# A decay tile of its own, and three loaded rows instead of four, in a Hymba step

## The chip, the cores and the metric

The kernel runs on one core of a Trainium2 chip. The metric is the device time of that core in microseconds (us); lower is better. Work is spread over the engines TensorE (PE), VectorE (DVE), ScalarE (ACT), GpSimd (POOL), and the DMA queues, of which SyncE (SP) issues most loads. Each engine runs its own instructions in a fixed order and waits on semaphores for the others.

## The reference

One inference step of a hybrid decoder layer. The input (1024 tokens of a new sequence, and 8 single tokens of running ones) is RMS-normalised and projected once; half of the channels go through a gated linear recurrence (RG-LRU), the other half through a matrix-memory recurrence (mLSTM) with four heads; both are gated, joined, projected by w_out, added to the input and normalised. The part that matters here is the mLSTM, done in chunks of 128 tokens per head:

```
b = cumsum(lf);  D = b[t] - b[s] + ig[s]  for s <= t, else -inf
g = b + m;  m_t = max(g, max_s D);  w = exp(D - m_t)
P = w * (q k^T)                       # [128, 128] per head and chunk
num = P v + exp(g - m_t) * (q C)      # C: the head's state
den = sum_s P + exp(g - m_t) * (q n)
h = num / max(|den|, exp(-m_t))
C, n, m  -> carried to the next chunk
x = x + merged @ w_out;  y = rmsnorm(x)
```

All in float32.

## The kernel before

The program runs in stages: normalisation and the input projection (to about 540 us, overlapped later with the recurrence and the first mLSTM chunk), a transition in which w_out is loaded and split, then from about 690 us the mLSTM chunks with the output projection woven between them, and a tail. Matrix products are done in three passes: each operand is split into a rounded part and a residue, ACT copying the rounded part (L70) and DVE subtracting it (L71), so names come in pairs such as ph and pl; `mm3` (L64 to L66) issues the three matmuls. The instructions are issued through a scheduler that fixes the order on every engine when the kernel is built, by priorities, dependencies and the number of places (`bufs`) that each named tile has. An instruction that writes a tile waits until the last readers of that place are done.

There are 8 chunks with 4 heads, so 32 items n = 4c + h. For an item:

- `w_load(n)` (L1083 to L1087) loads one row of 128 numbers of d_alpha, repeated over 128 partitions, into a place of tile W; the load is on SP's queue.
- `m_load(n)` calls `w_load(n + 1)`, and loads qk (two places) and vt (two places).
- `m_k(n)` (from L1103) makes the decay matrix from the row: one DVE instruction adds the per-token term be_t and applies the causal mask (L1109), and ACT takes the Exp (L1110), both in place in W. From the second chunk on it also splits q (qh, ql) and the head's state Cf (Ch, Cl).
- `m_a(n)` makes the scores on PE (L1129, L1131), k scaled (kh on ACT L1137, kl on DVE L1139), the product pf of scores and W (L1138, DVE), and its parts ph and pl.
- `m_b(n)` does the products with the state and with v; hh is read from PSUM by ACT (L1185, from ps_qp) and completed by DVE (L1192); Cf is updated by DVE (L1190).
- `m_g(n)` multiplies by the output gate (L1205 to L1208); `m_n(c)` (L1215 to L1218, then the `rsqrt` helper with ACT's Sqrt at L187) makes the four scales ms of a chunk; `m_zg(c)` applies them on ACT (L1226); `m_z(c, pair)` transposes two heads on PE into the bank of ps_s or ps_qp (L1235), multiplies by the gate z on DVE (L1238) and splits the result into mh and ml.
- `out_part` is the output projection of a chunk: `mm3` with rh, rl (recurrence half) and mh, ml (mLSTM half) into ps_o, then y is added (L1360), squared and summed (L1361), normalised (L1303, L1304, L187, L1310) and stored.

The main loop weaves these. `fill(k)` issues k pieces of `out_part`; in each item the order is `m_a(n)`, `so_load(n)`, `m_g(n - 1)`, `m_load(n + 2)` and then, by head (cut to the calls):

```
if h == 0:   m_n(c - 1); fill(2); m_k(n + 1); fill(1); m_b(n); fill(1)
elif h == 1: m_zg(c - 1); fill(1); m_k(n + 1); fill(1); m_z(c - 1, 0)
             m_b(n); fill(1); m_z(c - 1, 1); fill(1)
else:        fill(1); m_k(n + 1); fill(2); m_b(n); fill(1)
```

After the loop the last chunk's `m_n`, `m_zg` and `m_z` follow, with what is left of the projection, and `last_tile`. Tiles ps_s, ps_qp and ps_tr have one place in PSUM each, qh, ql, Ch and Cl one in SBUF.

Of the kernel before, what the change touches and what calls it, by code (L numbers as in the profile page):

```python
# [9 lines left out]
F32 = mybir.dt.float32  # L10
# [3 lines left out]
ALU = mybir.AluOpType  # L14
# [3 lines left out]
P = 128  # L18
# [6 lines left out]
L = 128  # L25
# [24 lines left out]
def hymba_kernel(  # L50
# [7 lines left out]
    V, A, G, TE = nc.vector, nc.scalar, nc.gpsimd, nc.tensor  # L58
# [9 lines left out]
    def split(hi, lo, src):  # L68

        A.copy(hi, src)  # L70
        V.tensor_tensor(lo, src, hi.bitcast(F32), op=ALU.subtract)  # L71
# [10 lines left out]
    def const(shape, name, dt=F32):  # L82
        return cpool.tile(shape, dt, tag=name, name=name)
# [30 lines left out]
    maskT = const([P, P], "maskT")  # L114
# [12 lines left out]
    be_t = const([P, NCH, NH], "be_t")  # L127
# [914 lines left out]
    mx = {}  # L1042

    def m_open1():

        fpr["es"].close()
        mx["p"] = mp = es_m.enter_context(tc.tile_pool(name="f_m1", bufs=1, reuse_waits="tile"))
        mx["Cf"] = [mp.tile([P, 2, 258], F32, tag=f"Cf{h}", name=f"Cf{h}") for h in range(NH)]
        mx["v"] = vhl = [mp.tile([P, 258], F32R, tag=f"v{n}", name=f"v{n}") for n in "hl"]
        V.memset(vhl[0][:, 256:257].bitcast(F32), 1.0)  # L1050
        V.memset(vhl[0][:, 257:258].bitcast(F32), 0.0)
        V.memset(vhl[1][:, 256:258].bitcast(F32), 0.0)
        w_load(0)
        m_load(0)
        m_load(1)
        so_load(0)
        so_load(1)
# [11 lines left out]
    def m_load(n):  # L1069
        if n >= 4 * NCH:  # L1070
            return
        c, h = n // 4, n % 4
        ts_ = slice(c * L, (c + 1) * L)
        w_load(n + 1)
        qk = mx["p"].tile([P, 4, L], F32, tag="qk", name="qk", bufs=2)
        ld(qk, d_qk[h][:, :, ts_].rearrange("m p t -> p m t"))
        vt = mx["p"].tile([P, 256], F32, tag="vt", name="vt", bufs=2)
        ld(vt, d_v[h][ts_, :])
        it[n] = {"qk": qk, "vt": vt}

    Ws = {}

    def w_load(n):  # L1083
        if n < 4 * NCH:
            c, h = n // 4, n % 4
            Ws[n] = mx["p"].tile([P, L], F32, tag="W", name="W", bufs=4)
            ld(Ws[n], d_alpha[h:h + 1, c * L:(c + 1) * L].rearrange("o t -> (o t)").partition_broadcast(P))  # L1087

    sos = {}
# [13 lines left out]
    def m_k(n):  # L1103
        if n >= 4 * NCH:
            return
        c, h = n // 4, n % 4
        d = it[n]
        W = d["W"] = Ws.pop(n)
        V.scalar_tensor_tensor(W, W, be_t[:, c, h:h + 1], maskT, op0=ALU.add, op1=ALU.min)  # L1109
        A.activation(W, W, AF.Exp)  # L1110
        if c == 0:
            return
        qh = mx["p2"].tile([P, 2, L], F32R, tag="qh", name="qh")
        ql = mx["p2"].tile([P, 2, L], F32R, tag="ql", name="ql")
        split(qh, ql, d["qk"][:, 0:2, :])
        if c > 0:
            d["Ch"] = mx["p2"].tile([P, 2, 258], F32R, tag="Ch", name="Ch")
            d["Cl"] = mx["p2"].tile([P, 2, 258], F32R, tag="Cl", name="Cl")
            split(d["Ch"], d["Cl"], mx["Cf"][h])
        d["qh"], d["ql"] = qh, ql  # L1120

    def m_a(n):
# [14 lines left out]
        A.mul(kh, kn, de_t[:, c, h:h + 1])  # L1137
        V.scalar_tensor_tensor(pf, S, 1.0 / 16.0, d["W"], op0=ALU.mult, op1=ALU.mult)  # L1138
        V.scalar_tensor_tensor(kl, kn, de_t[:, c, h:h + 1], kh.bitcast(F32), op0=ALU.mult, op1=ALU.subtract)  # L1139
# [13 lines left out]
    def m_first(n):  # L1153

        def a():
            if n > 0:
                m_g(n - 1)
            if 0 < n < NH - 1:
                so_load(n + 1)
            m_k(n)  # L1160
            m_a(n)
            if n + 2 < NH:
                m_load(n + 2)

        def b():
            for kb, kv in enumerate(m_kv(n, ("qp", "s"))):
                V.tensor_copy(mx["Cf"][n][:, kb, :], kv)
        def c():
            pv = ps("qp", [P, 258])
            mm3(pv, it[n]["ph"], it[n]["pl"], *mx["v"], True, True)  # L1170
            hh = mx["p"].tile([P, 257], F32, tag="hh", name="hh", bufs=5)
            V.tensor_copy(hh, pv[:, 0:257])
            it[n]["hh"] = hh
            if n == NH - 1:
                m_g(n)
        return [a, lambda: None, b, c]
# [307 lines left out]
    while bg or late:  # L1484
        pop_bg()
    work.extend([out_part(0, 0, 0), out_part(0, 1, 0), out_part(1, 0, 0), out_part(0, 0, 1), out_part(0, 1, 1),
                 out_part(1, 1, 0)])
    m_k(4)
    fill(2)
    wo_split(12, 13)  # L1490
# [7 lines left out]
    for n in range(4, N):  # L1498
        c, h = n // 4, n % 4
# [15 lines left out]
        if h == 0:  # L1515
            m_n(c - 1)
            fill(2)
            m_k(n + 1)
            fill(1)
            if c == 1:  # L1520
                next(dend)
            m_b(n)
            fill(1)
        elif h == 1:
            m_zg(c - 1)
            fill(1)
            m_k(n + 1)
            fill(1)
            m_z(c - 1, 0)
            m_b(n)  # L1530
            fill(1)
            m_z(c - 1, 1)
            fill(1)
            if c < last:
                o_load(c + 1)
        else:
            fill(1)
            tail()
            m_k(n + 1)
            fill(2)  # L1540
            m_b(n)
            fill(1)
# [45 lines left out]
```

## Time and profile before

| | |
|---|---|
| median of three runs | 945.27 us |
| the three runs | 943.84, 945.27, 946.10 us |
| the profiled execution | 946.52 us |
| its span in the profile | 944.8 us |
| instructions | 15,352 |
| granted TensorE clock, mean | 0.998 |

The span runs from the first to the last instruction of the profile; the time of that execution is 1.7 us longer. In rows of the timeline the columns are the start and the duration in us, the engine, the line, the operation, output and inputs by the program's names, the tile's shape, how many instructions the row holds, and in brackets how long the engine had been idle and what ended the idle time. PEld is the loading of weights into PE, which overlaps with matmuls. The profiler models the ends of matmuls; their starts are measured. In a list of waits the columns are the total in us, the number of waits, and the longest.

### The profile page before, as it was taken

Reading aid. Unit: us, or ns where it says so; the run is one execution under the profiler, and the core shown is the slowest. Engines: PE = TensorE matmul, PEld = TensorE weight load, DVE = VectorE, ACT = ScalarE, POOL = GpSimd, SP = SyncE. Lnnn points to the kernel's source line nnn. Section 1 sums busy time; section 2 is a strip of 40 time slices with the busy share of each in tenths; the row PEclk is TensorE's granted clock in tenths of the full one; section 3 lists DMA queues with packets and bytes.
Section 4 is the critical chain, followed back from the end, with each engine's and each line's share of the span. In section 5 each row is a group of like instructions: output and inputs, shape, how many; then the busy total and the mean of one; then the engine's idle time right before and its main releaser. Section 6 shows DMA issues by size and latency. Waiting matters only on the chain.

```text
span 944.8 us, 15352 instructions
## 1 busy us (share of the span) xinstructions
PE 921.0 (97%) x5350; PEld 760.6 (81%) x5350; DVE 711.8 (75%) x1465; ACT 587.5 (62%) x1052; POOL 145.6 (15%) x259
## 2 busy tenths in 40 slices
PE   9999999999999999999999999998899999999996
PEld 7897767777787987777789898876578888888886
DVE  6875898889798877988797867668857675677753
ACT  7653457778677757667578774465636456556532
POOL 1111112112112121211122221010101000000110
PEclk9999999999999999999999999999999999999999
DMA  6611447356746464545657362426963564464461
GB/s 196 207 40 44 134 141 258 110 185 204 243 144 207 157 207 167 173 148 188 200 173 247 124 210 95 151 112 201 306 207 114 149 185 122 140 187 140 132 92 45
DMA packets 131383, 153.19 MB, mean 162 GB/s; under 512 B 15816, under 2 KB 110056, under 8 KB 131298
## 3 DMA queue, kind: packets, MB, share of 16 engines
q1 hardware_dynamic: 113578, 96.34, 34.2%
q0 software_dynamic: 17728, 55.87, 16.5%
q8 instruction: 42, 0.69, 0.3%
q14 instruction: 35, 0.29, 0.1%
HBM read 100.59 MB, written 51.65 MB: 161 GB/s over the span
## 4 chain that ended last, share of the span: by engine, by line
PE 78%; DVE 9%; DMA 7%; issue 2%; ACT 2%; SPq 1%; POOL 0%; DVEq 0%; ACTq 0%; POOLq 0%
PE ps_o L66 12%; PE ps_o L64 12%; PE ps_o L65 12%; PE ps_kv L64 10%; PE ps_kv L65 9%; PE ps_kv L66 9%; DMA W<-d_alpha 3%; PE ps_tr L236 3%; DMA oraw<-in_w_out_dram 2%; DVE wl L71 1%; PE ps_s L1129 1%; PE ps_qp L956 1%; PE ps_s L789 1%; DMA x<-in_x_prompt_dram 1%; PE ps_tr L789 1%
## 5 line engine op out<-in xcount | busy, mean ns | idle before, releaser
L71 DVE TENSOR_TENSOR wl<-raw,wh 128x1024 fp32r<-128x1024 f32 x91 | 111.1, 1221 | 27.1 <-ACT wh L70 17.9
L70 ACT CAST wh<-raw 128x1024 fp32r<-128x1024 f32 x91 | 95.3, 1048 | 56.3 <-PE ps_o L65 23.4
L64 PE MATMUL ps_kv<-cb_hi,wh 128*128 128x512 f32 x320 | 128.0, 400 | 2.0 <-ACT wh L70 1.6
L66 PE MATMUL ps_kv<-cb_hi,wl 128*128 128x512 f32 x320 | 125.2, 392 | 0.0
L65 PE MATMUL ps_kv<-cb_lo,wh 128*128 128x512 f32 x320 | 125.1, 391 | 0.0
L64 PE MATMUL ps_o<-cb_hi,wh 128*128 128x512 f32 x240 | 95.2, 396 | 1.0 <-ACT wh L70 1.0
L66 PE MATMUL ps_o<-cb_hi,wl 128*128 128x512 f32 x240 | 93.8, 392 | 0.0
L65 PE MATMUL ps_o<-cb_lo,wh 128*128 128x512 f32 x240 | 93.6, 390 | 0.0
L64 PEld LDWEIGHTS ps_kv<-cb_hi,wh 128*128 128x128 f32 x320 | 60.1, 188 | 23.9 <-issue 3.4
L65 PEld LDWEIGHTS ps_kv<-cb_lo,wh 128*128 128x128 f32 x320 | 60.2, 188 | 13.2 <-issue 1.7
L66 PEld LDWEIGHTS ps_kv<-cb_hi,wl 128*128 128x128 f32 x320 | 60.1, 188 | 13.0
L64 PEld LDWEIGHTS ps_o<-cb_hi,wh 128*128 128x128 f32 x240 | 45.1, 188 | 12.8 <-issue 2.5
L64 PE MATMUL ps_kv<-wh,cb_hi 128*128 128x256 f32 x192 | 55.4, 288 | 0.0
L65 PE MATMUL ps_kv<-wl,cb_hi 128*128 128x256 f32 x192 | 54.3, 283 | 0.0
L66 PE MATMUL ps_kv<-wh,cb_lo 128*128 128x256 f32 x192 | 54.3, 283 | 0.0
L66 PEld LDWEIGHTS ps_o<-cb_hi,wl 128*128 128x128 f32 x240 | 45.0, 188 | 10.6 <-DVE pf L1138 0.8
L66 PE MATMUL ps_o<-wo,ml 128*128 128x512 f32 (+1 forms) x136 | 52.1, 383 | 1.4 <-DVE ml L71 1.4
L64 PE MATMUL ps_o<-wo,rh 128*128 128x512 f32 (+1 forms) x136 | 53.3, 392 | 0.0
L65 PEld LDWEIGHTS ps_o<-cb_lo,wh 128*128 128x128 f32 x240 | 45.1, 188 | 9.9 <-issue 0.8
L64 PE MATMUL ps_o<-wo,mh 128*128 128x512 f32 (+1 forms) x136 | 52.9, 389 | 0.0
L66 PE MATMUL ps_o<-wo,rl 128*128 128x512 f32 (+1 forms) x136 | 51.6, 381 | 0.4 <-DMA rl<-d_rm 0.4
L65 PE MATMUL ps_o<-wo,rh 128*128 128x512 f32 (+1 forms) x136 | 51.6, 380 | 0.0
(481 smaller groups left out, 2530.9 us busy)
## 6 DMA issues: line engine op xcount, KB each, us to landing
raw<-in_w_in_dram SPq DMA_DIRECT2D x55, 512.0 KB
Cb<-in_state_mlstm_C_dram SPq DMA_DIRECT2D x32, 256.0 KB
out_dram<-Cb POOLq DMA_DIRECT2D x32, 256.0 KB, 4.7
qk<-d_qk SPq DMA_DIRECT2D x32, 256.0 KB
oraw<-in_w_out_dram SPq DMA_DIRECT2D x16, 512.0 KB
d_qk<-s POOLq DMA_DIRECT2D x24, 256.0 KB, 4.2
d_x<-s POOLq DMA_DIRECT2D x16, 256.0 KB, 2.6
zsr<-d_y SPq DMA_DIRECT2D x16, 256.0 KB
```

Source lines behind the costliest of these rows:

```text
L64: TE.matmul(out, ah, bh, start=first, stop=False, skip_group_check=True)
L65: TE.matmul(out, ah, bl, start=False, stop=False, skip_group_check=True)
L66: TE.matmul(out, al, bh, start=False, stop=last, skip_group_check=True)
L70: A.copy(hi, src)
L71: V.tensor_tensor(lo, src, hi.bitcast(F32), op=ALU.subtract)
L236: TE.matmul(pz[32 * g:32 * g + 32, :], hnd[:, NB * k:NB * k + 32], raws[u, k // 4][:, k % 4, :], start=k < 4, stop=k >= 4, skip_group_chec ...
L789: TE.matmul(pg, w[:, n, :], st["xx"][n], start=k == 0, stop=k == 1)
L956: TE.matmul(pq[32 * g:32 * g + n, 0:256], q, ds_["C", h * NB + bb][:, kb, :], start=b == 1, stop=b == NB - 1, skip_group_check=True)
L1129: TE.matmul(S, qk[:, 2 + kb, :], qk[:, kb, :], start=kb == 0, stop=kb == 1)
```

## The change

The addition and mask (L1109) no longer write into the place of W that the row was loaded to, but into a tile of its own, We, with one place; Exp then works in place in We, and the product pf reads We. The loaded rows have three places instead of four, so that the memory taken is the same. `d["W"]` is now the tile We.

```diff
@@ w_load @@
-            Ws[n] = mx["p"].tile([P, L], F32, tag="W", name="W", bufs=4)
+            Ws[n] = mx["p"].tile([P, L], F32, tag="W", name="W", bufs=3)
             ld(Ws[n], d_alpha[h:h + 1, c * L:(c + 1) * L].rearrange("o t -> (o t)").partition_broadcast(P))
@@ m_k @@
         c, h = n // 4, n % 4
         d = it[n]
-        W = d["W"] = Ws.pop(n)
-        V.scalar_tensor_tensor(W, W, be_t[:, c, h:h + 1], maskT, op0=ALU.add, op1=ALU.min)
+        W = d["W"] = mx["p"].tile([P, L], F32, tag="We", name="We")
+        V.scalar_tensor_tensor(W, Ws.pop(n), be_t[:, c, h:h + 1], maskT, op0=ALU.add, op1=ALU.min)
         A.activation(W, W, AF.Exp)
```

The scheduler builds the order of every engine anew from this.

## The prediction

> **What bounds the kernel now.** I read the page from the top: busy shares first, then the chain that ended last, then the waits of the one tile that the change touches.
>
> ```profile
> PE 921.0 (97%) x5350; PEld 760.6 (81%) x5350; DVE 711.8 (75%) x1465; ACT 587.5 (62%) x1052; POOL 145.6 (15%) x259
> ...
> PE 78%; DVE 9%; DMA 7%; issue 2%; ACT 2%; SPq 1%; POOL 0%; DVEq 0%; ACTq 0%; POOLq 0%
> ```
>
> TensorE (PE) is busy for 97% of the span and carries 78% of the chain. So time can be won only where PE stands still, or after it has ended. The view of the tile W lists the three instructions that write it, and the idle time ahead of them:
>
> ```profile
> L1087 SPq DMA_DIRECT2D W<-d_alpha x32: 319/382/1342, 547.9 to 880.8; - x32
> L1109 DVE SCALAR_TENSOR_TENSOR W<-W,be_t,maskT x32: 333/351/353, 555.1 to 884.4; 128x128 f32<-128x128 f32 x32
> L1110 ACT ACTIVATE W<-W x32: 293/310/313, 557.3 to 884.7; 128x128 f32<-128x128 f32 x32
> ...
>   DMA W<-d_alpha: 45.0, 21
>   DVE W L1109: 32.9, 18
> ```
>
> VectorE (DVE) stands for 45.0 us ahead of 21 of the 32 additions (L1109) until the row of W has landed, and ScalarE (ACT) for 32.9 us ahead of the Exp (L1110). Both engines work in order, so everything behind them stands too. What of this reaches PE? The windows of the mLSTM stage, one line each (columns: window, length, busy us of PE, PEld, DVE, ACT, POOL, then clock, DMA share, GB/s), and PE's wait in the same stretch:
>
> ```profile
> 690.00:722.00 32.00, 31.88 (x174) 25.84 (x173) 22.23 (x63) 17.34 (x46) 2.70 (x5) 1.00 0.52 155
> 722.00:755.00 33.00, 32.48 (x188) 28.06 (x187) 21.15 (x66) 17.59 (x46) 2.17 (x4) 1.00 0.48 146
> 755.00:788.00 33.00, 32.65 (x187) 27.99 (x186) 22.58 (x70) 18.86 (x51) 2.18 (x4) 1.00 0.53 152
> 788.00:821.00 33.00, 32.25 (x187) 27.71 (x185) 21.39 (x65) 18.53 (x49) 2.18 (x4) 1.00 0.53 152
> 821.00:854.00 33.00, 32.96 (x192) 28.58 (x189) 22.92 (x72) 18.86 (x50) 2.17 (x4) 1.00 0.52 152
> 854.00:888.00 34.00, 34.00 (x195) 29.52 (x194) 23.08 (x73) 19.55 (x51) 2.18 (x4) 1.00 0.49 148
> ```
> ```profile
> PE ps_o L66 <- DVE ml L71: 1.4, 3, 0.7
> ```
>
> From 690 to 888 PE lacks 0.12 + 0.52 + 0.35 + 0.75 + 0.04 = 1.78 us of being busy, and 1.4 us of its waiting is for one product, ml. The last window lacks nothing. One such place, in the timeline:
>
> ```profile
> 803.14 0.35 DVE L1109 SCALAR_TENSOR_TENSOR W<-W,be_t,maskT 128x128 f32<-128x128 f32 x1 [3.81 <-DMA W<-d_alpha]
> 804.75 0.68 DVE L71 TENSOR_TENSOR ml<-z,mh 128x512 fp32r<-128x512 f32 x1
> ```
> ```profile
> 804.34 0.40 PE L65 MATMUL ps_o<-wo,mh 128*128 128x512 f32 x1
> 805.49 0.50 PE L66 MATMUL ps_o<-wo,ml 128*128 128x512 f32 x1 [0.75 <-DVE ml L71]
> 805.82 0.39 PE L64 MATMUL ps_o<-wo,mh 128*128 128x512 f32 x1
> 806.05 0.40 PE L65 MATMUL ps_o<-wo,mh 128*128 128x512 f32 x1
> ```
>
> DVE waits 3.81 us, until 803.14, for a row of W that no product needs yet. The residue ml stands behind it, and PE waits for ml. The printed busy time of matmuls overlaps: they follow one another every 0.23 us (805.82 to 806.05) though each is 0.40 long. So the true loss is read from starts: 804.34 to 805.49 is 1.15, that is 0.92 beyond the step, and the restart (0.33 to the next) takes 0.10 more. I went through PE's starts from 690 to 888 in this way. Six gaps stand directly behind a DVE or ACT queue held by W: 0.28 (at 699.9), 0.79 (737.1), 0.34 (764.1), 0.44 (771.0), 1.02 (804.3), 0.20 (831.6), together 3.07 us.
>
> **The change part by part.** Both built orders can be laid side by side. The number of instructions is the same (32 additions, 32 Exps, 32 loads) apart from two table loads of ACT. The addition now writes a place of its own, of which there is one. So it can't run before the previous item's product pf (L1138) has read that place: the order on DVE becomes pf(n), kl(n), addition (n+1), and ACT's Exp follows ph(n). Before, the additions ran up to four items ahead of their product, and each took its row right after its load had been issued.
>
> *DVE's and ACT's waits.* A row's load in the old order, and the addition that takes it:
>
> ```profile
> 780.79 0.38 SPq L1087 DMA_DIRECT2D W<-d_alpha  x1
> ```
> ```profile
> 784.00 0.35 DVE L1109 SCALAR_TENSOR_TENSOR W<-W,be_t,maskT 128x128 f32<-128x128 f32 x1 [2.52 <-DMA W<-d_alpha]
> 797.15 0.28 DVE L1138 SCALAR_TENSOR_TENSOR pf<-ps_s,W 128x128 f32<-128x128 f32 x1
> ```
>
> From issue to addition there were 3.2 us, and the data had just come. With three loaded places, the load of row n+3 starts when the addition of item n frees a place, about where pf(n-1) freed it before, so loads are issued at about the same times; but now the row is taken two items later. A load issued at 780.8 is then used just behind the pf at 797.15: 16 us instead of 3.2. All 45.0 us of DVE's wait should go, and ACT's 32.9 with it. Of that, 3.07 us reaches PE. Bounds: nothing (if those gaps have another cause behind them) and -3.07; the windows' idle time, 1.78, lies between. I take the upper end, because each of the six gaps has the stalled queue directly ahead of its releaser, and in the old windows with only a small gap or none PE runs at 32.96 of 33 and 34.00 of 34.
>
> *The addition itself.* The same operation on the same shape, 0.351 us, in another place: 0, as its two reads and one write are the same in number. The wait that it adds is on pf, its own engine's instruction two ahead; behind it stand pl and z. Nothing on DVE is freed later than it.
>
> *ACT's table loads in the loop.* The Sqrt of L187 and the Exp need different tables:
>
> ```profile
> 789.54 1.28 ACT L187 ACT_TABLE_LOAD   x1
> 790.83 0.21 ACT L187 ACTIVATE ms<-ms 128x4 f32<-128x4 f32 x1
> ...
> 799.28 0.41 ACT L70 CAST qh<-qk 128x256 fp32r<-128x256 f32 x1 [0.52 <-ACT so L1208]
> ...
> 800.64 0.47 ACT L1185 ACTIVATE hh<-ps_qp,gi_t 128x257 f32<-128x257 f32 x1
> ```
> ```profile
> 801.62 0.60 PE L1235 MATMUL ps_qp<-idF,hh 128*128 128x128 f32 x4
> ```
>
> Each chunk loads both, as before, but Exp's load moves from the first head's item (behind L187) to the second's, behind ph. There it stands ahead of qh, Ch, mh and hh (L1185), and PE needs hh done before the transposes at 801.62, which use the same bank. In the new order pf of that item, now at 797.15, comes about 1.1 us earlier, because the 1.28 us load that qh and the chain behind it had ahead of them in the first head's item is gone; pf, kl and the addition then end near 797.2. From there to the end of hh: load 1.28, Exp 0.31, qh to the start of hh as in the rows (799.28 to 800.64) 1.36, hh 0.47, 3.4 us: 800.6. That is 1.0 us ahead of the need: cost 0. If this cover is gone, see the second rival.
>
> *The tail.* The last chunk now has an Exp after its Sqrt as well, so one more Sqrt table is loaded at the end, ahead of L187, where nothing follows to make up for it:
>
> ```profile
> 920.50 0.19 ACT L187 ACTIVATE ms<-ms 128x4 f32<-128x4 f32 x1
> 921.57 1.71 ACT L1226 ACTIVATE hh<-hh,ms 128x256 f32<-128x256 f32 x4 [0.30 <-DVE ms L194]
> ```
> ```profile
> 921.95 1.41 DVE L1310 SCALAR_TENSOR_TENSOR y<-y,fms,gf 128x512 f32<-128x512 f32 x2
> 923.90 0.69 DVE L1238 TENSOR_TENSOR z<-ps_s,z 128x512 f32<-128x512 f32 x1 [0.54 <-PE ps_s L1235]
> ```
> ```profile
> 923.26 0.60 PE L1235 MATMUL ps_s<-idF,hh 128*128 128x128 f32 x4
> 926.04 0.48 PE L66 MATMUL ps_o<-wo,ml 128*128 128x512 f32 x1
> ```
>
> The scaling by ms (L1226) would start at about 922.9 instead of 921.57. Its first two of four end near 923.8, so the transposes wait some 0.5 us from 923.26. DVE does the two L1310 in between, until about 924.7, so z starts 0.8 late and the first ml matmul some 0.7 after one 256-wide matmul is moved up. PE takes part of that in the wait at the transposes, not on top of it. I take +0.6; bounds 0 and the whole load, +1.28. The Trainium skill ("ScalarE: Activation LUTs", section "What ACT_TABLE_LOAD costs") gives every switch 1.28 us for the load and 1.38 us of drain, and its rule, to batch functions by table set, speaks against this change. By that price the tail would cost up to 1.4 us more and the sum would be about -1.1 instead. The trace disagrees on the drain: Sqrt starts 1.29 us after its load began.
>
> *The transition* (620 to 690). One load of W moves from ahead of four loads of w_out rows (oraw) to behind that of rl, and PE waits there for oraw:
>
> ```profile
> PE ps_tr L1269 <- DMA oraw<-in_w_out_dram: 2.7, 3, 1.3
> ```
>
> Issuing a load of W takes SP 0.38 us (its row above); out of oraw's way it can give that, in front of something else it can cost it: 0, bounds -0.4 and +0.4. The other moves on PE, SP and GpSimd (y's stores and loads alternate) release nothing that PE waits for.
>
> *Sum:* -3.07 + 0 + 0.6 + 0 = -2.5 us. The profiled execution took 946.5 us (span 944.8); the three runs have a median of 945.27. The difference holds for either: 944.0 against the profile, **942.8** against the median, -0.26%. What a measurement of this kernel can tell from no change is about 0.2%, 1.9 us.
>
> **The rivals.** *Within 0.2%.* The gaps close only by the 1.78 us that the windows show idle, and the tail pays its whole 1.28: -0.5, 944.8. For it: DVE's 45.0 us of waiting already leave PE almost untouched, and the ml gaps are only three of the listed waits. Against it: starts, not busy time, tell what PE lost.
>
> *Slower: the table loads lie on the path.* The place is Exp's load in the second head's item. Suppose that item's pf comes no earlier than 797.15. In the new order L1205 and L1207 stand ahead of it and pl ahead of the addition, so by my estimate the addition ends some 1.6 us later, at 798.8. Then hh ends at 802.2, 0.6 after the transposes want the bank, and PE waits in each of the six chunks that have them in this item (+3.6). With the tail in full (+1.28) and the ml gaps closed (0.79 + 0.44 + 1.02 = 2.25 saved) that is +2.6: 947.9. It decides where the addition of that item ends later than 798.2 on this scale, 1.0 us later than I expect. For it: the load now stands on the chain from pf to hh, where it didn't. Against it: DVE loses its waits in the item before too.
>
> *Slower: one place for the result.* The addition can't run ahead any more, so a late row stalls pf itself. The ml gaps recur every 33.3 to 33.9 us, a chunk of four items, so pfs stand some 8.4 us apart, and addition, table load and Exp take 0.35 + 1.28 + 0.31 = 1.94 of it. Only a row later than the other 6.4 costs anything. If one in each of seven chunks were that late, at the mean of the old waits (45.0 / 21 = 2.1 us), it would be +15, about 960. But rows would have to take 16 us and more. The Trainium skill ("Trainium Kernel Development and Optimization", Best Practices) asks for double buffers to overlap transfers with work; here the transfer keeps three places and only the result has one.
>
> *The change does nothing* (PE's gaps stay where they are, with other causes): 945.3 to 945.9.
>
> **How the numbers follow.** Forecast (-1.9 to -3.5): 0.57. Within 0.2%, with the case of no effect: 0.26. Slower: 0.17, of which 0.13 for the table loads and 0.04 for the single place. So faster 0.57, same 0.26, slower 0.17. The low end takes the whole gain, no cost in the tail and the transition's 0.4, less the spread of the runs' lowest (943.84): 941.0. The high end reaches through the "within" case into the slower one's near half: 947.4. That leaves out about 0.07 below and 0.10 above.
>
> **What would show it.** In the new profile: the wait of L1109 on the DMA of W falls from 45.0 us to under 5; PE's waits on ml fall from 1.4 to about 0; the windows between 690 and 888 are full to within 0.3 us each; L187 has one table load more, right before its last 128x4 instruction, and the tail's transposes wait 0.3 to 0.8 us behind it. I am wrong if PE waits on hh (L1185) at the ps_qp transposes in each chunk, if pf waits for the Exp, or if the 3 us come back as new waits of PE elsewhere.

## The result, and the profile after

| | before | changed |
|---|---|---|
| median of nine runs | 944.92 us | 940.55 us |
| lowest and highest | 943.75, 946.17 | 938.96, 942.77 |
| profiled execution, span | 946.52, 944.8 | 939.56, 937.8 |

The ratio is 0.9948, 95% interval 0.9936 to 0.9961: faster by 0.5%, 4 to 5 us. The forecast was -2.5 us, 942.8, with a low end of 941.0. The direction was right, and so was the mechanism in the chunks; the forecast gain is a little over half of the measured one, and the measured time lies below the low end.

The page of the changed kernel: busy time by engine, and the chain by engine.

```profile
PE 918.5 (98%) x5350; PEld 760.6 (81%) x5350; DVE 712.1 (76%) x1465; ACT 590.5 (63%) x1054; POOL 145.6 (16%) x259
...
PE 82%; DVE 6%; DMA 4%; issue 3%; ACT 2%; SPq 1%; POOL 0%; DVEq 0%; ACTq 0%; POOLq 0%
```

The number of instructions is the same on every engine, but for two more on ScalarE (1054 instead of 1052), the table loads. What is gone is waiting: DMA had 7% of the chain and has 4%, DVE 9% and has 6%. The view of the tile We (the addition, and the idle time ahead of its instructions):

```profile
L1109 DVE SCALAR_TENSOR_TENSOR We<-W,be_t,maskT x32: 332/344/349, 553.5 to 898.8; 128x128 f32<-128x128 f32 x32
...
  DVE We L1109: 4.8, 7
```

The line of before "DMA W<-d_alpha: 45.0, 21" has no successor: VectorE never waits for a row. ScalarE's wait for the addition fell from 32.9 to 4.8 us. The windows of the chunks, same columns as before:

```profile
722.00:755.00 33.00, 33.00 (x192) 28.88 (x192) 22.89 (x70) 19.23 (x51) 2.17 (x4) 1.00 0.53 152
755.00:788.00 33.00, 33.00 (x192) 28.88 (x191) 22.86 (x70) 19.23 (x52) 2.37 (x5) 1.00 0.50 152
788.00:821.00 33.00, 33.00 (x191) 28.86 (x190) 22.87 (x70) 19.23 (x52) 2.42 (x5) 1.00 0.53 152
821.00:854.00 33.00, 33.00 (x191) 28.82 (x189) 22.91 (x70) 19.23 (x52) 2.25 (x5) 1.00 0.50 152
```

TensorE is busy without a gap in these windows, and its list of waits from 690 us to the end is empty. To measure what that is worth, I used the same mark in every chunk, the transposes into ps_s (L1235). Two neighbours of before, then the same two of the changed kernel:

```profile
797.97 0.63 PE L1235 MATMUL ps_s<-idF,hh 128*128 128x128 f32 x4
831.99 0.63 PE L1235 MATMUL ps_s<-idF,hh 128*128 128x128 f32 x4
```
```profile
792.85 0.60 PE L1235 MATMUL ps_s<-idF,hh 128*128 128x128 f32 x4
825.59 0.60 PE L1235 MATMUL ps_s<-idF,hh 128*128 128x128 f32 x4
```

A period of 34.02 became 32.74 us. From the first to the seventh transposes it is 201.11 us before and 197.69 after, -3.4. In this way the time can be cut into pieces that add up, and it shows where the rest went: see the table further on.

### The profile page after: what moved, and what is told of

Read it like the earlier page. It is cut to its first block, busy times and chain, and to the rows that moved or that the text cites. A ratio compares the mean times of both kernels' runs of the same rounds, so it can differ in the third digit from the quotient of the medians.

```text
span 937.8 us, 15396 instructions
## 1 busy us (share of the span) xinstructions
PE 918.5 (98%) x5350; PEld 760.6 (81%) x5350; DVE 712.1 (76%) x1465; ACT 590.5 (63%) x1054; POOL 145.6 (16%) x259
## 4 chain that ended last, share of the span: by engine, by line
PE 82%; DVE 6%; DMA 4%; issue 3%; ACT 2%; SPq 1%; POOL 0%; DVEq 0%; ACTq 0%; POOLq 0%
PE ps_o L64 14%; PE ps_o L66 13%; PE ps_o L65 13%; PE ps_kv L64 9%; PE ps_kv L65 9%; PE ps_kv L66 9%; PE ps_tr L236 2%; PE ps_s L1129 2%; DMA oraw<-in_w_out_dram 1%; DVE wl L71 1%; PE ps_qp L956 1%; PE ps_qp L65 1%; PE ps_qp L64 1%; PE ps_qp L66 1%; PE ps_s L1131 1%
```

## The experiments

**1. The changed kernel and the kernel before, profiled again.** No edit. One profile each can't tell a kernel's property from a chance of that execution, so four more of each were taken.

> The changed kernel once more, to tell what of its gain is its own and what is one execution. In the first profile of it 2.2 us of the 7.0 us by which its span is shorter stand before 540 us, where the built orders of the two kernels are the same, and 1.0 us behind the last instruction. Theory A (waits on the row, as predicted, -3.1 in the chunks and +0.4 in the tail, and something in the transition on top): a ratio of 0.9950 to 0.9965, about 941 to 942, and again no wait of TensorE between 690 and 888 us. Theory B (the gain is only the 3.1 - 0.6 of the forecast, the rest is chance): 0.9968 to 0.9980, about 942.5.

> The kernel before, profiled once more, to tell how much of its loss is the same in every execution. Measured from one row to another, the first profile has 129.6 us from the first score matmul (L1129) to the first transposes (L1235), and chunk periods of 34.29, 33.90, 33.31, 34.02, 32.78, 32.81 us where the changed kernel has 32.75 in both of its profiles from the second period on. Theory A (the loss comes from rows that are late by different amounts): a sum of the six periods again well over six times 32.75, by 2 to 5 us, but spread over other chunks; first stretch 128 to 130. Rival (the loss in a chunk is fixed by the order): the same six periods within 0.1 us.

> The kernel before, a third profile. In the changed kernel the six chunk periods from the first to the seventh transposes take 197.65 and 197.69 us in two executions; in the kernel before they took 201.1 and 205.2. Theory V (the loss in the chunks differs from execution to execution, since it hangs on when each row lands, and the prediction took the loss of one execution for the mean): over this and the next two profiles the sum lies between 199 and 206 us and differs by over 0.5 us between them, and its mean exceeds 197.65 by 4 to 5.5. Rival (201.1 is typical, and the rest of the gain of 4.7 us is in the transition): sums within 0.5 us of 201.1, first stretch 1.5 us over 128.1.

> The kernel before, a fourth profile; expectations as for the third.

> The kernel before, a fifth profile; expectations as for the third.

> The changed kernel, a third profile. If its transition is shorter by its order: 127.8 to 128.4 us again in this and the next two. If that was chance: between 128 and 131.4, with a mean near 129.5. The last store's wait: 1.8 us again in all if it hangs on the kernel, 1.8 to 2.7 if on chance. Chunk periods 32.75 from the second on.

> The changed kernel, a fourth profile; expectations as for the third.

> The changed kernel, a fifth profile; expectations as for the third.

The second timing gave 939.87 us, ratio 0.9944 (0.9928 to 0.9960): the gain is the kernel's own, and a little more than theory A said. Pieces of the five executions of each, in the order in which they were taken, read from rows like those above. "Transition" is from the first score matmul (L1129) to the first transposes, "six periods" to the seventh, "seventh" to the eighth, "tail" from there to the issue of the last two stores (L1408, one row), "last store" from there to the end of the execution's time.

| us | before | changed | difference of means |
|---|---|---|---|
| time | 946.52, 949.99, 944.50, 945.81, 946.79 | 939.56, 941.30, 940.47, 939.58, 939.39 | -6.7 |
| up to the first score matmul | 566.87, 564.88, 566.52, 566.45, 565.40 | 565.27, 567.17, 565.61, 565.62, 565.57 | -0.2 |
| transition | 129.60, 130.92, 128.16, 129.75, 131.37 | 128.14, 128.04, 128.76, 127.88, 127.70 | -1.9 |
| six periods | 201.11, 205.21, 200.86, 200.68, 201.09 | 197.69, 197.65, 197.65, 197.66, 197.65 | -4.1 |
| seventh period | 25.68 in all | 25.96 or 25.97 | +0.3 |
| tail | 16.54, 16.57, 16.57, 16.54, 16.54 | 16.69, 16.66, 16.65, 16.65, 16.69 | +0.1 |
| last store | 6.72, 6.73, 6.71, 6.71, 6.71 | 5.81, 5.81, 5.83, 5.81, 5.81 | -0.9 |

The second execution of before, at 949.99 us, is slower than any of the nine timed runs above and in one chunk far out of line. The ten executions come from several chips, not in pairs from one, while each timed comparison was made on one chip. Rows of the second execution of before in the chunk that is out of line, VectorE and then TensorE:

```profile
802.79 0.35 DVE L1109 SCALAR_TENSOR_TENSOR W<-W,be_t,maskT 128x128 f32<-128x128 f32 x1 [5.00 <-DMA W<-d_alpha]
```
```profile
805.13 0.50 PE L66 MATMUL ps_o<-wo,ml 128*128 128x512 f32 x1 [1.93 <-DVE ml L71]
```

VectorE's wait for the row is 5.00 us instead of 3.81, and TensorE's wait behind it 1.93 instead of 0.75: the same mechanism, more of it. Something comes on top. The window behind that wait, and one in the transition of the fifth execution of before, behind a wait of 2.58 us for w_out (the third column from the end is the granted clock):

```profile
806.00:809.30 3.30, 3.30 (x9) 2.56 (x8) 2.73 (x8) 1.79 (x5) 0.00 (x0) 0.50 0.41 114
```
```profile
664.50:667.90 3.40, 3.08 (x16) 0.59 (x16) 3.08 (x4) 1.68 (x2) 0.00 (x0) 0.50 0.67 244
```

The granted clock is 0.50 there and 1.00 in the windows on both sides. TensorE loses up to 1.7 us in such a stretch of 3.4 us (an estimate, half of it), on top of the wait. The second execution of before has one in the transition too (from 659.2); the first, third and fourth have none in the transition or the chunks, nor has any of the five of the changed kernel. Not every wait of that length is followed by one: in experiment 2 a wait of 2.50 us, until 765.37, is not. The gain of the change doesn't come from the clock: among the timed runs with a mean clock of 0.998 or more, 42 of the kernel before have a mean of 945.2 us and 10 of the changed kernel one of 940.0.

Without the second execution of before the six periods differ by 3.3 and the time by 5.8 us. So theory V (the loss in the chunks is very different from execution to execution) fell in the main: four of five lie within 0.5 us. The loss in the chunks was 3.0 to 3.5 us, with an outlier of 7.6. What the forecast lacked is mostly in two other rows: the transition and the last store.

**2. In place, three places: half of the change.**

```diff
-            Ws[n] = mx["p"].tile([P, L], F32, tag="W", name="W", bufs=4)
+            Ws[n] = mx["p"].tile([P, L], F32, tag="W", name="W", bufs=3)
```

> Half of the change: three places, but the decay matrix still in place. Its table loads and its order of additions and products are nearly those of the changed kernel (an addition behind each product, three items ahead of its own product), but each addition takes its row straight after the load that the product ahead of it set free. Theory A (what counts is the time between the issue of a row's load and the addition): VectorE waits 45 us or more for the rows, TensorE keeps its gaps at ml, 944 to 947 us, ratio 0.999 to 1.002. Rival (what counts is that additions no longer stand several in a row, or where the Exp's table is loaded): as fast as the changed kernel, 940 to 942.

959.83 us, ratio 1.0152 (1.0133 to 1.0172): 15 us slower than before, more than either theory said. The tile W and TensorE's waits from 690 us on:

```profile
  DMA W<-d_alpha: 62.7, 27
  DVE W L1109: 53.5, 23
```
```profile
PE ps_s L1235 <- DVE ms L1205: 11.4, 5, 3.0
```

Table loads, number of places for rows and nearly the whole order are those of the changed kernel; only the row's load waits for the product, not for the addition. Theory A holds in kind, not in size: I had expected the gaps to stay, and a period grew from about 33.5 to 36 or 37 us. A part of this is the clock: within 1 us behind waits of 2.42, 2.18 and 2.98 us for ms it fell to 0.50 for 3.4 us, three times, up to 5 us together by the estimate above. So three places alone are a loss of 15 us, and the own tile turns it into a gain of 5.

**3. In place, one place.** VectorE's order of additions and products is then exactly that of the changed kernel.

```diff
-            Ws[n] = mx["p"].tile([P, L], F32, tag="W", name="W", bufs=4)
+            Ws[n] = mx["p"].tile([P, L], F32, tag="W", name="W", bufs=1)
```

> One place, in place: VectorE's order is that of the changed kernel (an addition behind each product, one item ahead), and the number of loaded places is as in the one-place kernel with its own tile; only the row's load has to wait for the product instead of the addition, so it is issued just ahead of the addition that uses it. Theory A (time between issue and addition): VectorE waits 3 us in nearly all of 28 items, 60 to 100 us in all, and TensorE waits in every chunk; 955 to 965 us. Rival (the order alone): 940 to 945.

980.16 us, ratio 1.0364 (1.0339 to 1.0390), 35 us slower than before and beyond the 955 to 965 of theory A. The tile W, and TensorE's waits from 690 us on:

```profile
  DMA W<-d_alpha: 83.1, 30
  DVE W L1109: 76.4, 22
```
```profile
PE ps_qp L1235 <- ACT hh L1185: 20.0, 7, 8.6
PE ps_s L1235 <- ACT hh L1226: 4.9, 5, 1.9
```

The order of additions and products is thus not what makes the changed kernel fast. With a late row, that order is the worst of all, because the Exp with its table load stands ahead of hh (L1185). This is the place of the prediction's second rival, with 20.0 us of waits here; the changed kernel stays out of it because its rows are there in time. About 15 of the 35 us are in the seventh period alone (41.10 instead of 25.68 us), where two rows came 11.1 and 10.5 us after their issue. The first of them, its load and its addition:

```profile
919.91 0.38 SPq L1087 DMA_DIRECT2D W<-d_alpha  x1
```
```profile
931.05 0.35 DVE L1109 SCALAR_TENSOR_TENSOR W<-W,be_t,maskT 128x128 f32<-128x128 f32 x1 [9.46 <-DMA W<-d_alpha]
```

Why these two were so late isn't shown. The clock takes part here too: the profile's mean is 0.985. How much isn't shown either, since a timed run with a mean of 0.992 still took 979.12 us.

**4. Own tile, one loaded place** (the edit is to the changed kernel).

```diff
-            Ws[n] = mx["p"].tile([P, L], F32, tag="W", name="W", bufs=3)
+            Ws[n] = mx["p"].tile([P, L], F32, tag="W", name="W", bufs=1)
```

> The decay matrix in its own tile, but only one place for a loaded row instead of three. A row's load is issued when the previous addition has read the place, one item (about 8 us) ahead of its use. Theory A: 8 us are more than the 3 to 5 us that a row took to land, so nothing changes: wait of VectorE on rows under 5 us in all, 940 to 942 us. Rival (three places are needed to hide the load): VectorE waits 1 us or more per item for rows, 20 us or more in all, products late, 944 or slower.

944.23 us, ratio 0.9991 (0.9981 to 1.0001). By the time alone the rival would have won. The profile says otherwise. Two rows of the chunks, a row's load on SP and the addition that takes it, 8 us later and without a wait; then the wait on rows in the whole run:

```profile
788.13 0.32 SPq L1087 DMA_DIRECT2D W<-d_alpha  x1
```
```profile
796.10 0.34 DVE L1109 SCALAR_TENSOR_TENSOR We<-W,be_t,maskT 128x128 f32<-128x128 f32 x1
```
```profile
  DMA W<-d_alpha: 2.8, 1
```

The six periods take 197.65 us, as in the changed kernel. The loss is elsewhere: the transition takes 131.04 us. There, SP's queue, SP's wait for the row load, and what TensorE waited for:

```profile
665.00 0.33 SPq L1251 DMA_DIRECT2D oraw<-in_w_out_dram  x1
668.40 0.33 SPq L1087 DMA_DIRECT2D W<-d_alpha  x1
668.83 0.44 SPq L1251 DMA_DIRECT2D oraw<-in_w_out_dram  x1
```
```profile
SPq L1087 <- DVE ql L71: 3.3, 1, 3.3
```
```profile
PE ps_tr L1269 <- DMA oraw<-in_w_out_dram: 3.8, 2, 3.2
```

A row load that can't start yet, since its place isn't free, stood for 3.3 us at the head of SP's queue with a load of w_out behind it. TensorE then waited 3.2 us for w_out.

**5. The same with that one load issued later.**

```diff
-        w_load(n + 1)
+        if n == 6:
+            w_load(6)
+        if n != 6 - 1:
+            w_load(n + 1)
```

> The own tile with one loaded place, which took 944.2 us, but the one load of a row that stood between two loads of w_out rows in the transition is issued one item later, so that it stands behind rl as in the changed kernel. Theory T (in the one-place kernel that load waits 3.3 us for its place at the head of SP's queue and holds a w_out load behind it, for which TensorE waits 3.2 us): TensorE's longest wait on oraw falls from 3.2 to about 1.3 us, the stretch from the first score matmul to the first transposes from 131.0 to 128 us, time 940 to 941.5. Rival (one loaded place costs in other ways, or the transition's loss is chance): 943 to 945.

940.53 us, ratio 0.9952 (0.9940 to 0.9965): 3.7 us less than experiment 4 from moving one load, as theory T says. The profiled execution took 944.27 us, far above its kernel's median, and had 131.01 us in the transition. Yet at the place in question it agrees with T. The transposes of w_out behind the held load in experiment 4, then the same ones and the next here (where the line is three further down):

```profile
676.06 2.99 PE L1269 MATMUL ps_tr<-oraw,mBd 128*32 128x512 f32 x16 [3.22 <-DMA oraw<-in_w_out_dram]
```
```profile
673.84 1.92 PE L1272 MATMUL ps_tr<-oraw,mBd 128*32 128x512 f32 x16
683.42 1.75 PE L1272 MATMUL ps_tr<-oraw,mBd 128*32 128x512 f32 x8 [2.06 <-DMA oraw<-in_w_out_dram]
```

The wait of 3.22 us is gone. This execution lost its time one group later, by another wait for w_out, 2.06 us, with the clock at 0.50 for 3.4 us behind it. The two versions of experiment 8 differ by the same move of one load and repeat the gain, 943.16 and 940.63 us.

**6. The transition's row load taken off SP's queue in the kernel before.**

```diff
-            ld(Ws[n], d_alpha[...])
+            (stq if n == 8 else ld)(Ws[n], d_alpha[...])
```

> The kernel before with one load, the row that stands between w_out loads in the transition, issued on GpSimd's queue instead of SP's; the orders of the other engines stay. Theory T (that load waits at the head of SP's queue and holds w_out loads behind it, and this is the changed kernel's gain in the transition): transition 128.0 to 128.5 us, ratio 0.997 to 0.999. Rival (the transition differs from execution to execution with the arrival of w_out, whatever the order): 128 to 131.5 as in the kernel before, ratio 0.999 to 1.001. Chunk periods and the last store's wait (2.7 us) unchanged by both.

944.86 us, ratio 0.9991 (0.9977 to 1.0006); transition 128.99 us, between the two means of the table. The time doesn't decide, but SP's waits in the profile of before, from 657 to 672 us, say why little could be won:

```profile
SPq L1257 <- DVE wl L71: 2.7, 1, 2.7
```
```profile
SPq L1087 <- DVE pf L1138: 2.3, 1, 2.3
```

The row's load waits 2.3 us for its place at the head of the queue (1.5 to 3.7 in the five executions). But the load of w_out behind it then waits 2.7 us more for a place of its own (2.7 to 3.6), so the row's load holds nothing back there. The chunks stayed as they were (200.54). The last store's wait did not stay as expected, see below.

**7. Two places for the result, two for rows.**

```diff
-            Ws[n] = mx["p"].tile([P, L], F32, tag="W", name="W", bufs=3)
+            Ws[n] = mx["p"].tile([P, L], F32, tag="W", name="W", bufs=2)
...
-        W = d["W"] = mx["p"].tile([P, L], F32, tag="We", name="We")
+        W = d["W"] = mx["p"].tile([P, L], F32, tag="We", name="We", bufs=2)
```

> Two places for the result and two for loaded rows: additions may run two items ahead of their product, and a row's load is issued two items ahead of its addition (the place is free once the addition two before has read it). Theory A (time between issue and addition): no waits on rows, chunk periods 32.75, 940 to 941.5. Rival (a single place for the result held the changed kernel back): faster than the changed kernel by over 1 us; rival (additions must not stand ahead of their product): 944 or slower.

940.41 us, ratio 0.9948 (0.9936 to 0.9961), six periods 197.68: theory A; neither rival. A single place for the result costs nothing here.

**8. The tail's table load taken out,** first with one loaded place as in experiment 4, then with the load moved as in experiment 5. The last two items' matrices are made in their own rows' places ahead of `m_n` of the last chunk but one:

```diff
+        if n == N - 4:
+            for i in (N - 2, N - 1):
...
+                V.scalar_tensor_tensor(W, W, be_t[...], maskT, op0=ALU.add, op1=ALU.min)
+                A.activation(W, W, AF.Exp)
```

> As the kernel with its own tile and one loaded place, and the decay matrices of the last two items are made earlier, ahead of the Sqrt of the chunk before, in two places of their own: the last chunk's second pair of table loads is gone, and with it the one in the tail. Theory A (the tail's extra load costs 0.4 to 0.6 us): 0.4 to 0.6 us faster than the kernel before it in this list. Rival (the load is hidden or moves to something else): the same as that kernel within 0.2. If making them early holds up ScalarE or VectorE: slower by up to 1 us.

> A version that should beat both: own tile, one loaded place, the transition's row load behind rl, and the last two items' decay matrices made ahead of the last Sqrt but one, so that the tail has no table load. Theory: 0.4 us better than the one-place kernel with the late load of this list, that is 0.4 us in the tail (from the last transposes to the end 16.5 instead of 16.7, the chunk before 25.7 instead of 26.0); 939.5 to 941. If the two rows loaded long ahead hold something up in the transition: 941 to 943.

943.16 us, ratio 0.9971 (0.9958 to 0.9985), and 940.63 us, ratio 0.9954 (0.9938 to 0.9971). In both profiles the seventh period is 25.68 and the tail 16.54 us, as in the kernel before, instead of 25.96 and 16.7: the tail's table load costs the changed kernel 0.4 us, as expected. In the time it can't be told: the first is 1.1 us below experiment 4, the second 0.1 above experiment 5, by the medians. No version tried beats the changed kernel by more than the measurement can tell; those of experiments 5 and 7 and the second of 8 equal it, the one of experiment 5 with a single loaded place.

## Why the prediction was right or wrong

*The waits on the row* (all 45.0 us gone): right, none is left. The lead is even longer than I wrote. A load set free by the addition of item n is taken three additions later, which at 8.2 us each (32.75 / 4) is about 24 us, where I counted 16. Experiments 2, 3 and 4 show that this time is what counts: in the three kernels that work in place a row is mostly taken 3 to 5 us after its load is issued, and VectorE waits 45, 63 and 83 us; 8 us of lead left no such wait and cost nothing in the chunks. What the waits cost in the end, 3.3, 15 and 35 us, hangs on the order of the instructions and on the clock as well. The Trainium skill ("DMA: Bandwidth & Descriptors", section "Rules for kernel authors") says to issue a transfer early and to wait for it late; the runs agree, and add that a place freed late makes the issue late, whatever the number of places.

*What of it reaches TensorE* (3.07 us): right in mechanism, and in size for four of five executions (3.0 to 3.5 us). Reading the gaps from starts and not from busy time was the better choice: the windows' idle time gave 1.78. The sum missed the execution in which a row came later still (7.6).

*The table load in the second head's item* (0): right, with half of the cover that I counted. The changed kernel's rows on ScalarE, VectorE and TensorE:

```profile
792.46 1.28 ACT L1110 ACT_TABLE_LOAD   x1 [0.67 <-DVE We L1109]
...
795.49 0.47 ACT L1185 ACTIVATE hh<-ps_qp,gi_t 128x257 f32<-128x257 f32 x1
```
```profile
791.19 0.28 DVE L1138 SCALAR_TENSOR_TENSOR pf<-ps_s,We 128x128 f32<-128x128 f32 x1
...
792.04 0.35 DVE L1109 SCALAR_TENSOR_TENSOR We<-W,be_t,maskT 128x128 f32<-128x128 f32 x1
```
```profile
796.47 0.60 PE L1235 MATMUL ps_qp<-idF,hh 128*128 128x128 f32 x4
```

hh ends at 795.96, 0.5 us ahead of the transposes at 796.47; I had said 1.0. TensorE is 5.15 us earlier here than in the old trace, so pf came 0.8 us earlier against it, not 1.1. The rival that priced the loss of this cover at 947.9 did not come true, but experiment 3 shows waits at its place.

*The tail* (+0.6, bounds 0 and 1.28): right in kind. Measured +0.4: 0.3 in the seventh period and 0.1 behind it. ScalarE, VectorE and TensorE in the tail of the changed kernel:

```profile
914.13 1.28 ACT L187 ACT_TABLE_LOAD   x1
915.43 0.20 ACT L187 ACTIVATE ms<-ms 128x4 f32<-128x4 f32 x1
...
916.50 1.71 ACT L1226 ACTIVATE hh<-hh,ms 128x256 f32<-128x256 f32 x4 [0.77 <-DVE ms L194]
```
```profile
916.41 1.42 DVE L1310 SCALAR_TENSOR_TENSOR y<-y,fms,gf 128x512 f32<-128x512 f32 x2
917.93 0.69 DVE L1238 TENSOR_TENSOR z<-ps_s,z 128x512 f32<-128x512 f32 x1
```
```profile
917.06 0.44 PE L1235 MATMUL ps_s<-idF,hh 128*128 128x128 f32 x2
...
917.46 0.44 PE L1235 MATMUL ps_s<-idF,hh 128*128 128x128 f32 x2
```

The Sqrt follows 1.30 us after the load began. The drain of 1.38 us per switch that the prediction cited from the Trainium skill ("ScalarE: Activation LUTs", section "What ACT_TABLE_LOAD costs") doesn't show, here either; the measurement decides. The transposes did not wait 0.3 to 0.8 us as I said: the first pair goes at once and one matmul of the recurrence half stands between the pairs.

*The transition* (0, bounds -0.4 and +0.4): **the step that failed.** I priced it by the 0.38 us that the issue of one row load takes, and said that the other moves release nothing that TensorE waits for. Measured was -1.9 in the mean of five (128.2 to 131.4 against 127.7 to 128.8), -1.6 without the far execution. TensorE's listed waits in this stretch, for w_out, for rl and for ACT's rounded parts wh, are 4.4 to 6.4 us before and 3.6 to 4.9 in the changed kernel, 5.6 and 4.3 in the mean; the stretches at half the clock in two of the five executions of before add about 0.7 to its mean, an estimate. Together that is about the difference. What a row load in SP's queue can cost is the time for which it waits for its place with w_out's loads behind it: experiment 4 shows 3.3 us at the head of the queue and 3.2 us of TensorE's time. In the kernel before this is not the cause, as experiment 6 shows. Why TensorE waits less for w_out in the changed kernel stays open. The own tile alone doesn't bring it: the profile of experiment 7, which has that too, shows 5.8 us of waits and a transition of 129.61.

*The end* (no term at all): an omission besides. SP's wait for the last store to land, in before and after:

```profile
SPq L1583 <- DMA out_dram<-yg: 2.7, 1, 2.7
```
```profile
SPq L1583 <- DMA out_dram<-yg: 1.8, 1, 1.8
```

2.7 us in all five executions of before, 1.8 in all five of the changed kernel: 0.9 us. I have no cause for it.

*The sum* of the pieces, without the one far execution of before: -0.5 up to the first score matmul, where the built orders are the same, -1.6 transition, -3.3 periods, +0.4 in the seventh period and the tail, -0.9 last store, together about -5.9 for profiled executions; the timed runs say -4.4 by their medians and -4.9 by the ratio. The pieces that hardly differ between executions (-3.3, +0.4 and -0.9, together -3.8) leave 0.6 to 1.1 us of that for the transition and what stands ahead of it, by my estimate. Of the forecast's own terms, -3.07 and +0.6, the same pieces measured -3.3 and +0.4. The range's low end failed with the transition's bound, since it allowed 0.4 us there and nothing at the end. It was also added up wrongly: the whole gain and 0.4 us less than the median are 941.8, less than the lowest run 940.4, and 941.0 is neither; 940.4 would have held the measured 940.55, by luck, as the end wasn't in it. The rivals "within 0.2%" and "single place" are refuted, the second by experiment 7.

## What to carry to other kernels

When a loaded tile is overwritten in place, its place comes free only when the last product has read the result, so the next load starts late and more places only let the scheduler run further ahead; an own tile for the result frees the loaded place at the first read, and one such place then did as well in the chunks as three. Price a load in an in-order queue not by its issue but by what it holds back while it waits for its place; that is nothing where the load behind it would have to wait anyway. Look at the granted clock behind every longer wait of TensorE before the whole loss is put down to the wait. Before a gain of a few microseconds is summed from one trace, cut several executions at the same marks, from the first instruction to the last store: each piece has a spread of its own, and here the pieces without a term in the sum came to nearly as much as those with one.

## What the runs showed of the hardware

The wait for the last store belongs to the kernel, not to chance: 2.7 us in the kernel before and in place with three places, 1.8 in the changed kernel and in experiments 3, 5, 7 and both of 8, and 2.4 in experiment 4, though nothing near the last store was edited (experiment 8 takes a table load out of the tail). The difference also shows between profiles from one chip. With a single load of the transition issued by GpSimd instead of SP (experiment 6) it became:

```profile
SPq L1583 <- DMA out_dram<-yg: 2.3, 2, 1.9
```

Which property of the earlier transfers decides it is open.

A row of 64 KB took 3.2 us from issue to use in the trace of before when it was awaited at once, and in experiment 3 up to 5.2 us in the middle chunks (issued at 768.93, addition at 774.09, by the rows of its timeline) and 11.1 us in the last, so the lead that hides such a load has to be sized by the slow ones.

The granted clock in the transition and the chunks was 1.00 but for stretches of 3.4 us, or twice that, at 0.50: three in the two executions of before that experiment 1 names, one each in the transition of experiments 4 and 5, behind waits of 3.22 and 2.06 us, one of 6.8 us in that of the first version of experiment 8, three in the chunks of experiment 2, and seven in experiment 3, whose mean clock is 0.985. How long a wait has to be to bring one on isn't settled by these runs.
